# A decoder layer on one core: first values for all columns at once, the order of the last loads of v, and a last norm shared with TensorE

## The chip, the cores and the metric

The kernel runs on one core of one Trainium2 chip. The metric is the device time of one execution in microseconds (us); of several runs the median is given.

## The reference

One decoder layer on 256 tokens of width 2048, in float32. The weights are large, the tokens few.

```python
dq, dk, dv, sq, sk, sv = split(x @ w_in)              # 2048 x 6144
merged = concat(diff_attention(dq, dk, dv),           # 8 heads, rotary, two softmaxes
                stick_breaking_attention(sq, sk, sv)) # 8 heads
x = layer_norm(alpha * x + merged @ w_out)
x = layer_norm(alpha * x + peer_ffn(x))               # 16384 experts: gelu(x . u[e]), times v[e]
x = layer_norm(alpha * x + sigmoid(x @ w_gate) * (p @ w_proj))
```

`layer_norm` is `(x - mean) * rsqrt(var + eps) * g + b` over the 2048 columns.

## The kernel before, in words

**Layout.** P is 128 partitions, T 256 tokens, NT = 2 token tiles t, ND = 16 tiles k of the model's width d. `X` holds x transposed, tile by tile, as a high part and a low part (float32r each, side by side), so that a product in float32 precision is three fast products: `mm3` (L218) does hi x wh (L221), hi x wl (L222), lo x wh (L223), each 128x512.

**Weights.** Class `Stage` loads a weight tile `wf` with a DMA on SP's queue (`load`, L101), and splits it (`split`, L108): ACT casts the high part `wh` (L114), DVE subtracts to get the low part `wl` (L115). Buffers go round: 4 of `wf` and 4 pairs of `wh`, `wl` in the attention stage, each 1024 columns wide; a load waits until the buffer's last reader is done.

**First values.** The kernel begins with the values of the stick-breaking heads, `values(2, before=load_x)` (L370, L315): 1024 columns, c = 0 and then c = 1, 512 columns each. For each c, `gemm_N` (L225) goes over 8 pairs of d tiles; a load of 128x1024 holds both tiles of a pair for these 512 columns, and a pair gives 12 products. Two PSUM banks hold c's sums for the two token tiles, and ACT copies them out at the end of each c (L324). While c = 0 runs, x is loaded too: `load_x0` (L255) for tiles 0 and 1, one at a time, `load_x` (L261) for the later pairs; ACT makes the high part (L258, L264) and DVE the low one (L259, L265). The first pair of weights comes in two halves (`halves`, L118). All these DMAs stand in SP's queue: x tile 0, half of w, x tile 1, half of w, then x and w by pairs. `load_constants` follows c = 0.

**The middle.** Query and key projections (`proj`, `gemm_T`, L202 and L204) with attention in between, the output projection, the first norm, the expert queries (L214), then 128 blocks of u (`u_block`, L973) and twice 128 blocks of v (`v_block`, L1054), each block a 128x1024 or 128x2048 tile of weights. Beside them 200 gathers of expert rows run on POOL's DMA queue, and `gate_work` (L908) makes one-hot matrices: DVE compares, ACT scales (L929, L930), PE multiplies (L937, L938), DVE applies. The framework's scheduler places these pieces between the blocks; only what is passed to `keep` stays in program order.

**The end of v.** The last STAG = 6 blocks of v (three loads of 1 MB) are held and used j by j (L1150 to L1182), so that sums, transposes and statistics of the second norm fit in between. The loop at L1150 issues the held loads of v (`v_load`) and two loads of the gate's weights, the first after v's block 123, the second after 127. All share five buffers of 1 MB in the pool `sup`. `parts0` splits the gate's first weights (L1154). Then come the second norm (`ln_stats`, L477; POOL takes the reciprocal root, L482) and the gate's 4 column chunks. `gate_out` (L1256) loads the embedding through POOL's queue (L1260), applies the sigmoid (L1264), the product (L1265), the sum (L1266) and the statistics (L1269).

**The last norm.** `finish_stats` (L1272) combines the statistics; POOL takes the reciprocal root `rstd` (L1277). `pass1` (L1283) computes (x - mean) * g and `pass2` (L1288) x * rstd + b, both on DVE over column cuts, and after each piece of `pass2` SP issues the output's DMA (L1292). For token tile 1 this comes behind PE's last product, with cuts of 640, 640, 512 and 256 columns.

Of the kernel before, what the change touches and what calls it, by code (L numbers as in the profile page):

```python
# [9 lines left out]
F32 = mybir.dt.float32  # L10
# [9 lines left out]
P = 128  # L20
T = 256
NT = T // P
D = 2048
# [37 lines left out]
OHB = 5  # L61
STAG = 6
WF = 5

# [23 lines left out]
class Stage:  # L88
# [19 lines left out]
    def split(self, wf, c0, n=None):  # L108
# [7 lines left out]
        return wh, wl  # L116

    def halves(self, src, before):  # L118

        wf = self.wf_pool.tile([P, 1024], F32, name="wf", tag="wf", bufs=self.wf_bufs)  # L120
        for j in range(2):
            c = slice(j * 512, j * 512 + 512)
            before(j)
            self.nc.sync.dma_start(wf[:, c], src[:, c])
            yield self.split(wf, j * 512, 512)

# [36 lines left out]
def build(tc, a, out):  # L163
# [60 lines left out]

    def gemm_N(st, src, xt, pairs, pss, first=True, last=True, before=None):  # L225

        pairs = list(pairs)
        for i in pairs:
            if before and i:
                before(i)  # L230
            k = 2 * i
            parts = st.parts(src(i)) if i or not before else st.halves(src(i), load_x0)
            for wh, wl in parts:
# [21 lines left out]
    def load_x0(k):  # L255
        xf = sap.tile([P, T], F32, name="xf0", tag="xf0", bufs=2)
        nc.sync.dma_start(xf, a["xT"][:, k, :])
        nc.scalar.copy(X[:, k, :T], xf)  # L258
        nc.vector.tensor_tensor(X[:, k, T:], xf, Xf[:, k, :T], op=ALU.subtract)  # L259
# [54 lines left out]

    def values(base, before=None):  # L315
        v = cap.tile([P, NT, HEADS * HD], F32, name="v", tag="v", bufs=2)
        for c in range(2):
            pss = [pbank(pp, "ps_v") for _ in range(NT)]
            gemm_N(sa, lambda i: a["w_v"][base + c, i], X, range(ND // 2), pss,
                   before=before if c == 0 else None)  # L320
            if before and c == 0:
                load_constants()
            for t in range(NT):
                nc.scalar.copy(v[:, t, c * 512:(c + 1) * 512], pss[t])  # L324
        return v
# [43 lines left out]

    vs_ = values(2, before=load_x)  # L370
    for h in range(HEADS):
# [78 lines left out]

    vd_ = values(0)
    x1 = [x1p.tile([P, D], F32, name=f"x1_{t}") for t in range(NT)]
# [686 lines left out]
    for ia in range(SEG1, NIA - STAG):  # L1139
# [139 lines left out]

    def cuts(cut):  # L1280
        return [slice(*p_) for p_ in zip([0] + cut, cut + [D])]

    def pass1(t, cut, mv, rstd):  # L1283
        for s in cuts(cut):
            keep(nc.vector.scalar_tensor_tensor(x2[t][:, s], x2[t][:, s], mv[:, 0:1], gr3[:, s],
                                                op0=ALU.subtract, op1=ALU.mult))

    def pass2(t, cut, mv, rstd):  # L1288
        for s in cuts(cut):
            keep(nc.vector.scalar_tensor_tensor(x2[t][:, s], x2[t][:, s], rstd, br3[:, s],  # L1290
                                                op0=ALU.mult, op1=ALU.add))
            nc.sync.dma_start(out[t * P:(t + 1) * P, s], x2[t][:, s])  # L1292
# [83 lines left out]
    for c in range(NCH):  # L1376
        if c == NCH - 1:
            pass2(0, [512, 1024, 1536], *mr)
            gate_out(c, 1, ps_half, 256, 256)
            break  # L1380
# [19 lines left out]
        mr = finish_stats(0)  # L1400
        pass1(0, [512, 1024, 1536], *mr)
# [52 lines left out]
def _layout(inp):  # L1454
# [6 lines left out]
    def pairs(q, k):  # L1461
# [49 lines left out]
```

## Time and profile before

| | us |
|---|---|
| median of three runs (1776.26 to 1778.22) | 1777.45 |
| the profiled execution | 1776.11 |
| its span, first to last instruction | 1774.2 |
| PE busy | 1752.7 |
| first product on PE | 4.57 |
| first product of the query and key projections | 53.25 |
| last product of the gate ends | 1762.9 |

How to read it: times in the trace count from the span's start. PE is TensorE's products, PEld its weight loads, DVE VectorE, ACT ScalarE, POOL GpSimd; SPq, ACTq and POOLq are instructions that issue DMAs. A line of the timeline has the start, the duration, engine, source line, operation, output<-input, shapes, count, and in brackets the idle time before it and what ended it. A line of the chain has start, duration and what. In the list of waits stand the total, the number and the longest.

### The profile page before, as it was taken

How to read it: one execution, taken by the hardware profiler on the slowest of the kernel's cores; microseconds unless marked ns; L12 is line 12 of the kernel's file. 1: busy time of each engine (PE TensorE's matmuls, PEld its weight loads, DVE VectorE, ACT ScalarE, POOL GpSimd, SP SyncE). 2: the span in 40 equal slices, each digit the busy share in tenths (PEclk: the TensorE clock that was granted, in tenths of full speed). 3: DMA queues.
4: the chain of work that ended last, by engine and by line, in shares of the span. 5: the costliest groups of instructions: out<-in, count | busy, mean ns of one | idle time of the engine just before them, and what ended most of it. 6: DMA issues, size and time to landing. Idle time of an engine off the chain costs nothing.

```text
span 1774.2 us, 30337 instructions
## 1 busy us (share of the span) xinstructions
PE 1752.7 (99%) x12074; PEld 1647.6 (93%) x12074; DVE 1058.7 (60%) x1699; ACT 540.3 (30%) x1347; POOL 516.4 (29%) x554
## 2 busy tenths in 40 slices
PE   8999999999999999999999999999999999999997
PEld 6888888888889999999999999999999999999786
DVE  5565588664699877345655644876343433344686
ACT  5677468742110100104333313651000000000452
POOL 0143033105346227323333333333223232321000
PEclk9999999999999999999999999999999999999998
DMA  7544644576998999999999999999999999999671
GB/s 284 193 158 163 232 159 145 178 270 219 381 419 309 421 416 417 421 421 420 420 421 413 419 419 418 405 420 397 421 421 420 421 421 420 420 420 405 216 267 59
DMA packets 99822, 606.22 MB, mean 342 GB/s; under 512 B 12824, under 2 KB 14544, under 8 KB 35776
## 3 DMA queue, kind: packets, MB, share of 16 engines
q1 hardware_dynamic: 68368, 388.82, 55.4%
q0 software_dynamic: 30160, 213.10, 29.3%
q8 instruction: 95, 1.56, 0.4%
q10 hardware_dynamic: 1152, 2.36, 0.4%
q14 instruction: 47, 0.39, 0.1%
HBM read 598.36 MB, written 6.03 MB: 341 GB/s over the span
## 4 chain that ended last, share of the span: by engine, by line
PE 93%; DMA 4%; DVE 1%; ACT 0%; issue 0%; SPq 0%; POOL 0%; DVEq 0%; ACTq 0%
PE ps_v L1043 30%; PE ps_u L214 29%; PE ps_qk L202 7%; PE ps_q L214 6%; PE ps_qk L204 4%; DMA wf<-peer_u 2%; PE ps_v L222 2%; PE ps_v L223 2%; PE ps_gate L221 2%; PE ps_gate L223 2%; PE ps_gate L222 2%; PE ps_v L221 2%; DMA wf<-peer_v 1%; PE ps_mix L222 1%; PE ps_mix L223 1%; PE ps_mix L221 1%
## 5 line engine op out<-in xcount | busy, mean ns | idle before, releaser
L1043 PE MATMUL ps_v<-A,wf 128*128 128x156 f32 x4096 | 553.0, 297 | 1.2 <-DMA wf<-peer_v 1.1
L1043 PEld LDWEIGHTS ps_v<-A,wf 128*128 128x128 f32 x4096 | 545.0, 190 | 2.7 <-DMA wf<-peer_v 1.9
L214 PE MATMUL ps_u<-XF,wf 128*128 128x156 f32 x3904 | 528.2, 297 | 1.8 <-DMA wf<-peer_u 1.3
L214 PEld LDWEIGHTS ps_u<-XF,wf 128*128 128x128 f32 x3904 | 519.2, 190 | 3.1 <-ACT A L976 2.0
L841 DVE SCALAR_TENSOR_TENSOR y<-gb,ew,y 128x2048 f32<-128x2048 f32 x94 | 220.9, 2350 | 220.9 <-DMA gb<-v_rows,eig 220.7
L831 DVE SCALAR_TENSOR_TENSOR gb<-gb,xq 128x2048 f32<-128x2048 f32 x100 | 231.7, 2321 | 147.2 <-DMA gb<-u_rows,eig 147.1
L115 DVE TENSOR_TENSOR wl<-wf,wh 128x1024 fp32r<-128x1024 f32 (+1 forms) x199 | 212.7, 1090 | 110.5 <-ACT wh L114 98.9
L862 POOL COPY pace<-mark 1x1 f32<-1x1 f32 x200 | 108.2, 541 | 514.6 <-DMA mark<-c_iota 514.2
L114 ACT CAST wh<-wf 128x1024 fp32r<-128x1024 f32 (+1 forms) x199 | 172.1, 892 | 142.2 <-PE ps_yn L887 30.3
L202 PE MATMUL ps_qk<-X,wh 128*128 128x512 f32 x512 | 185.2, 401 | 0.0
L976 ACT ACTIVATE A<-ps_u 128x156 f32<-128x156 f32 x128 | 38.4, 300 | 433.6 <-PE ps_u L214 361.9
L864 POOL DMA_INDIRECT gb<-v_rows,eig x100 | 137.2, 1372 | 90.1 <-DVE y L841 54.7
L864 POOL DMA_INDIRECT gb<-u_rows,eig x100 | 122.1, 1221 | 126.3 <-DVE gb L831 67.2
L204 PE MATMUL ps_qk<-X,wl 128*128 128x256 f32 x512 | 145.7, 285 | 0.0
L929 ACT ACTIVATE hi<-eq,ghf 128x64 f16<-128x64 f16 x312 | 104.8, 336 | 45.1 <-DVE eq L923 42.2
L202 PEld LDWEIGHTS ps_qk<-X,wh 128*128 128x128 f32 x512 | 96.4, 188 | 21.9 <-issue 1.0
L214 PE MATMUL ps_q<-XF,wf 128*128 128x256 f32 x512 | 113.6, 379 | 0.6 <-DVE XF L509 0.6
L1104 ACT COPY x<-ps_y 128x256 f32<-128x256 f32 (+3 forms) x12 | 5.2, 439 | 346.3 <-DVE st L1103 346.1
L214 PEld LDWEIGHTS ps_q<-XF,wf 128*128 128x128 f32 x512 | 95.9, 190 | 13.1 <-DVE XF L509 0.8
L930 ACT ACTIVATE lo<-eq,glf 128x64 f16<-128x64 f16 x312 | 104.4, 335 | 0.0
L204 PEld LDWEIGHTS ps_qk<-X,wl 128*128 128x128 f32 x512 | 96.3, 188 | 2.5 <-issue 1.3
L947 DVE SCALAR_TENSOR_TENSOR A<-ps_G,A 128x30 f32<-128x30 f32 (+2 forms) x96 | 32.5, 368 | 45.0 <-PE ps_G L938 39.5
(261 smaller groups left out, 1801.0 us busy)
## 6 DMA issues: line engine op xcount, KB each, us to landing
wf<-peer_v SPq DMA_DIRECT2D x128, 1024.0 KB
wf<-peer_u SPq DMA_DIRECT2D x122, 1024.0 KB
wf<-w_qk SPq DMA_DIRECT2D x64, 512.0 KB
wf<-w_out SPq DMA_DIRECT2D x32, 512.0 KB
wf<-peer_wq SPq DMA_DIRECT2D x16, 1024.0 KB
wf<-ple_gate SPq DMA_DIRECT2D x16, 1024.0 KB
wf<-w_v SPq DMA_DIRECT2D x31, 512.0 KB
early<-peer_u SPq DMA_DIRECT2D x6, 1024.0 KB
```

The lines of the kernel that those rows point to most:

```text
L114: self.order(nc.scalar.copy(wh, src))
L115: self.order(nc.vector.tensor_tensor(wl, src, wh.bitcast(F32), op=ALU.subtract))
L202: nc.tensor.matmul(ps, wh[:, j * P:(j + 1) * P], xt[:, dt, :], start=dt == 0, stop=False)
L204: nc.tensor.matmul(ps[:, :T], wl[:, j * P:(j + 1) * P], xt[:, dt, :T], start=False, stop=dt == ND - 1)
L214: nc.tensor.matmul(ps[:, :T - t0], wf[:, dt * P:(dt + 1) * P], xt[:, dt, t0:], start=dt == 0, stop=dt == ND - 1)
L831: keep(nc.vector.scalar_tensor_tensor(g, g, 1.0, xq[i], op0=ALU.mult, op1=ALU.mult, accum_out=eact[i][:, j:j + 1]))
L841: keep(nc.vector.scalar_tensor_tensor(ys[i], g, ew[i][:, j:j + 1], ys[i], op0=ALU.mult, op1=ALU.add))
L862: keep(nc.gpsimd.tensor_copy(pace, mark))
L864: keep(nc.gpsimd.indirect_dma_start(out=g, out_offset=None, in_=a[kind], in_offset=bass.IndirectOffsetOnAxis(ap=eig[i][:, 0, j:j + 1], axi ...
L929: nc.scalar.mul(hi[:, j, :], eq[:, j, :], ghf[:, t])
L930: nc.scalar.mul(lo[:, j, :], eq[:, j, :], glf[:, t])
L1043: return nc.tensor.matmul(ps[:, (j % 2) * NDT:(j % 2 + 1) * NDT], vf[:, j * P:(j + 1) * P], W_of(ia), start=False, stop=ia == NIA - 1 and ...
```

## The change

Three places change.

1. `first_values` takes the place of `values(2, ...)`. It goes over the 16 d tiles once; for each it loads 128x1024 weights, all columns of that tile, from a new layout `w_sv`, and does the 12 products of both c into four PSUM banks (two of `pp`, two of `pt_`). x's tiles 0 and 1 are loaded through ACT's DMA queue, the weights and later pairs of x through SP's. Ahead of it, NZERO = 3 products of a zeroed part of M into a bank of its own go to PE. The constants follow tile 8, and the four copies of the sums stand at the end.
2. The gate's first two loads come after all held loads of v.
3. In the last norm of token tile 1, `pass1` goes over quarters, the last two first. For these two, PE computes `first_row.T @ b` (a row of b on all partitions; the same product is issued twice, and the second one starts the sum anew) and adds `diag(rstd) @ x`; ACT builds the diagonal, copies the sum out of PSUM and issues the output's DMA. `pass2` on DVE keeps the first two quarters. Token tile 0 keeps its four quarters.

In PE's order the four products with `first_row` stand behind the gate's last product; in POOL's order three loads of `gate_out` stand ahead of the second norm's reciprocal roots.

```diff
     def load_x0(k):
         xf = sap.tile([P, T], F32, name="xf0", tag="xf0", bufs=2)
-        nc.sync.dma_start(xf, a["xT"][:, k, :])
+        nc.scalar.dma_start(xf, a["xT"][:, k, :])
+        yield
         nc.scalar.copy(X[:, k, :T], xf)
         nc.vector.tensor_tensor(X[:, k, T:], xf, Xf[:, k, :T], op=ALU.subtract)
...
+    def first_values():
+        v = cap.tile([P, NT, HEADS * HD], F32, name="v", tag="v", bufs=2)
+        x0 = [load_x0(k) for k in range(2)]
+        for x in x0:
+            next(x)
+        nc.vector.memset(Mf[:, 0, :T], 0.0)
+        ps = pbank(pt_, "ps_zero", "o", 1)
+        for _ in range(NZERO):
+            nc.tensor.matmul(ps[:, :T], Mf[:, 0, :P], Mf[:, 0, :T], start=True, stop=True)
+        pss = [[pbank(pp, "ps_v") for _ in range(NT)],
+               [pbank(pt_, "ps_v", "s", 2) for _ in range(NT)]]
+        for k in range(ND):
+            if k == 0:
+                wf = sap.tile([P, 1024], F32, name="wf", tag="wf", bufs=4)
+                for c in range(2):
+                    nc.sync.dma_start(wf[:, c * 512:(c + 1) * 512],
+                                      a["w_sv"][0][:, c * 512:(c + 1) * 512])
+                next(x0[0], None)
+                parts = [sa.split(wf, c * 512, 512) for c in range(2)]
+            else:
+                if k > 1 and k % 2 == 0:
+                    load_x(k // 2)
+                wf = sa.load(a["w_sv"][k])
+                if k == 1:
+                    next(x0[1], None)
+                wh, wl = sa.split(wf, 0)
+                parts = [(wh[:, c:c + 512], wl[:, c:c + 512]) for c in (0, 512)]
+            for c in range(2):
+                for t in range(NT):
+                    mm3(pss[c][t], X, k, t, *parts[c], k == 0, k == ND - 1)
+            if k == ND // 2:
+                load_constants()
+        for c in range(2):
+            for t in range(NT):
+                nc.scalar.copy(v[:, t, c * 512:(c + 1) * 512], pss[c][t])
+        return v
...
-    vs_ = values(2, before=load_x)
+    vs_ = first_values()
...
-    held, gw = [], []
+    held = []
     for ia in range(NIA - STAG, NIA):
         held.append(v_load(1, ia))
-        if ia in (NIA - STAG + 1, NIA - 1):
-            gw.append(sg2.load(a["ple_gate"][0, len(gw)]))
+    gw = [sg2.load(a["ple_gate"][0, i]) for i in range(2)]
     parts0 = [sg2.split(gw[0], c * 512) for c in range(4)]
...
+    first_row = l2.tile([P, P], F32, name="first_row")
+    nc.gpsimd.memset(first_row, 0.0)
+    nc.gpsimd.memset(first_row[:1], 1.0)
...
-    mr = finish_stats(1)
-    pass1(1, [640, 1280, 1792], *mr)
-    pass2(1, [640, 1280, 1792], *mr)
+    psf = [pbank(pp, "ps_fin") for _ in range(2)]
+    for again in range(2):
+        for ps, s in zip(psf, quarters[2:]):
+            keep(nc.tensor.matmul(ps, first_row, br3[:, s], start=True, stop=not again))
+    mv, rstd = finish_stats(1)
+    diag = l3.tile([P, P], F32, name="diag")
+    keep(nc.scalar.mul(diag, ident, rstd))
+    pass1(1, quarters[2:] + quarters[:2], mv, rstd)
+    for ps, s in zip(psf, quarters[2:]):
+        keep(nc.tensor.matmul(ps, diag, x2[1][:, s], start=False, stop=True))
+        keep(nc.scalar.copy(x2[1][:, s], ps))
+        nc.scalar.dma_start(out[P:, s], x2[1][:, s])
+    pass2(1, quarters[:2], mv, rstd)
...
-        "w_v": _row_chunks(np.concatenate([dv, sv], axis=1)),
+        "w_v": _row_chunks(dv),
+        "w_sv": sv.reshape(ND, P, HEADS * HD),
```

More of the change, by code (lines that the diff above doesn't have):

```diff
@@ L62 @@
 STAG = 6
+NZERO = 3
 WF = 5
@@ L116, in split @@
         return wh, wl
[L118 to L125, printed above, removed]
     def parts(self, src):
@@ L223, in mm3, with gemm_N @@
         order(nc.tensor.matmul(ps, lo, wh, start=False, stop=stop))
-    def gemm_N(st, src, xt, pairs, pss, first=True, last=True, before=None):
+    def gemm_N(st, src, xt, pairs, pss, first=True, last=True):
         pairs = list(pairs)
         for i in pairs:
-            if before and i:
-                before(i)
             k = 2 * i
-            parts = st.parts(src(i)) if i or not before else st.halves(src(i), load_x0)
-            for wh, wl in parts:
+            for wh, wl in st.parts(src(i)):
                 for j in range(wh.shape[-1] // 512):
@@ L312, in load_constants2, with values @@
         nc.vector.tensor_scalar_mul(subg, subg, 1.0 - LAMBDA_INIT)
-    def values(base, before=None):
+    def first_values():
[34 more added lines that the diff above has]
+        return v
+    def values():
         v = cap.tile([P, NT, HEADS * HD], F32, name="v", tag="v", bufs=2)
@@ L318, in values @@
             pss = [pbank(pp, "ps_v") for _ in range(NT)]
[L319 to L322, printed above, removed]
+            gemm_N(sa, lambda i: a["w_v"][c, i], X, range(ND // 2), pss)
             for t in range(NT):
@@ L449, in diff_attention @@
         split_into(M, h, od, 0, T)
-    vd_ = values(0)
+    vd_ = values()
     x1 = [x1p.tile([P, D], F32, name=f"x1_{t}") for t in range(NT)]
@@ L1278, in finish_stats @@
         return mv, rstd
-    def cuts(cut):
-        return [slice(*p_) for p_ in zip([0] + cut, cut + [D])]
+    quarters = [slice(c * 512, (c + 1) * 512) for c in range(NCH)]
     def pass1(t, cut, mv, rstd):
-        for s in cuts(cut):
+        for s in cut:
             keep(nc.vector.scalar_tensor_tensor(x2[t][:, s], x2[t][:, s], mv[:, 0:1], gr3[:, s],
@@ L1288, in pass2 @@
     def pass2(t, cut, mv, rstd):
-        for s in cuts(cut):
+        for s in cut:
             keep(nc.vector.scalar_tensor_tensor(x2[t][:, s], x2[t][:, s], rstd, br3[:, s],
@@ L1377, in build @@
         if c == NCH - 1:
-            pass2(0, [512, 1024, 1536], *mr)
+            pass2(0, quarters, *mr)
             gate_out(c, 1, ps_half, 256, 256)
```

2 lines of the change are left out of this document (1 added, 1 removed).

## The prediction

> **What bounds the kernel now.** I read the page first: the busy shares and the chain of work that ended last.
>
> ```profile
> span 1774.2 us, 30337 instructions
> PE 1752.7 (99%) x12074; PEld 1647.6 (93%) x12074; DVE 1058.7 (60%) x1699; ACT 540.3 (30%) x1347; POOL 516.4 (29%) x554
> PE 93%; DMA 4%; DVE 1%; ACT 0%; issue 0%; SPq 0%; POOL 0%; DVEq 0%; ACTq 0%
> ```
>
> PE works for 1752.7 of 1774.2 us, and 93% of the chain is PE. So only two things can be gained: the 21.5 us in which PE is idle, and work that PE does too slowly. The second view is PE's list of waits, which says where that idle time is.
>
> ```profile
> PE ps_v L221 <- ACT wh L114: 4.9, 2, 4.6
> PE ps_u L214 <- DMA wf<-peer_u: 1.3, 3, 0.5
> PE ps_v L1043 <- DMA wf<-peer_v: 1.1, 1, 1.1
> PE ps_u L214 <- ACT A L976: 0.4, 1, 0.4
> ```
>
> The reader is to see how short it is: 4.9 us at the start, 1.1 us on one load of v, little else. The rest lies behind PE's last product, in the last norm. The change works at exactly these three places, so I take them one by one in the timeline and hold the other 1700 us to be unchanged.
>
> **Part 1, the first values.** The timeline and the chain of the first 12 us, then the first product of the next stage:
>
> ```profile
> 2.95 0.40 ACT L258 CAST X<-xf 128x256 fp32r<-128x256 f32 x1 [0.94 <-DMA xf<-xT]
> 1.18 0.42 SPq L124 DMA_DIRECT2D wf<-w_v  x1
> 3.90 0.62 ACT L114 CAST wh<-wf 128x512 fp32r<-128x512 f32 x1 [0.55 <-DMA wf<-w_v]
> 4.57 1.22 PE L221 MATMUL ps_v<-wh,X 128*128 128x512 f32 x2 [4.57 <-ACT wh L114]
> 6.18 0.62 ACT L114 CAST wh<-wf 128x512 fp32r<-128x512 f32 x1 [1.36 <-DMA wf<-w_v]
> 9.01 0.63 PE L222 MATMUL ps_v<-wl,X 128*128 128x512 f32 x1
> 9.44 0.63 PE L223 MATMUL ps_v<-wh,X 128*128 128x512 f32 x1
> 3.06 6.17 DMA wf<-w_v
> 9.26 1.04 ACT L114 CAST wh<-wf 128x1024 fp32r<-128x1024 f32 x1 [0.73 <-DMA wf<-w_v]
> 10.34 1.22 DVE L115 TENSOR_TENSOR wl<-wf,wh 128x1024 fp32r<-128x1024 f32 x1 [1.08 <-ACT wh L114]
> 11.62 0.51 PE L222 MATMUL ps_v<-wl,X 128*128 128x512 f32 x1 [0.33 <-DVE wl L115]
> 12.12 0.23 PE ps_v L223
> 53.25 0.39 PE L202 MATMUL ps_qk<-X,wh 128*128 128x512 f32 x1
> ```
>
> The phase has 192 products. The first twelve start 0.43 us apart (9.01 to 9.44), the later ones 0.23: PE begins at half rate and is at full rate when it comes back after 10.4. At 11.62 fourteen are issued; the other 178 take 53.25 - 11.62 = 41.63 us, 0.234 each. What decides is therefore when the third step can run: the second pair of d tiles is loaded in 6.17 us (issued 3.06, landed 9.23), cast in 1.04, its low part made in 1.22, and only then PE runs without a gap.
>
> How many bytes had to move for that comes from windows that begin at zero (the last two columns are the busy share of the DMA engines and GB/s):
>
> ```profile
> 0.00:6.15 6.15, 1.58 (x4) 1.25 (x5) 1.45 (x3) 2.61 (x4) 0.32 (x6) 1.00 0.59 157
> 0.00:9.23 9.23, 4.66 (x11) 3.65 (x12) 2.81 (x5) 3.85 (x6) 0.32 (x6) 1.00 0.69 215
> 0.00:8.20 8.20, 3.63 (x9) 2.81 (x10) 2.15 (x4) 3.52 (x6) 0.32 (x6) 1.00 0.66 201
> ```
>
> Up to the load that decides, 1.54 MB stand in the queue (two 128 KB tiles of x, two 256 KB halves of w, 256 KB of x, 512 KB of w). By 9.23 us 215 x 9.23 = 1.98 MB had moved: 0.45 MB of later loads ran beside it. In the new order twelve products need one d tile of all 1024 columns: 0.77 MB before the first tile is complete (two x, two halves of w), and 1.28 MB until the second tile's weights are there, since its x came with the first. With the same 0.45 MB beside it that is 1.73 MB; 201 x 8.20 = 1.65 MB had moved by 8.20, so it lands at about 8.4 (w's first issue also moves up from 1.18 to x's old place, which I count for nothing beyond that).
>
> From there: cast to 9.45, low part to 10.7, then the tile's last eight products, 8 x 0.234, to 12.6, and fourteen more tiles of twelve: 12.6 + 168 x 0.234 = 51.9. The two tiles behind it need 0.77 and 0.51 MB more at some 400 GB/s, less time than PE's 2.8 us for each, so they are not late. **The term is 53.25 - 51.9 = 1.35 us.** PE's first real product doesn't move: ACT now casts the weights first and x second, and w lands half a microsecond sooner, about 3.4 + 0.62 + 0.40 = 4.4 against 4.57.
>
> Ends for the unknown: if the load lands when it did (9.23), the sum is 0.5; if it lands when the queue has moved 1.28 MB and nothing beside it (7 us), PE is held by its own twelve products and the gain is 2.6.
>
> The **zero products** are three of 128x256 in fp32. The nearest row is the queries':
>
> ```profile
> L214 PE MATMUL ps_q<-XF,wf 128*128 128x256 f32 x512 | 113.6, 379 | 0.6 <-DVE XF L509 0.6
> ```
>
> 512 records are 256 products, so one is two records of 0.222 us at full rate, and at half rate, by the ratio 0.43 to 0.234, 0.82 us. Three take 2.5 us, from about 1.1 (after the memset) to 3.6: inside PE's idle 4.57 us, free. If they started over 0.9 us later they would push the first real one. What they can give is an earlier full rate. In my sum that matters little, since the load at 8.4 holds PE: at full rate from some 7 us on, PE has done its first tile by about 8.8 and waits.
>
> [...]
>
> Four copies of v instead of two now stand at the end of the phase on ACT, four times 0.59 by this row:
>
> ```profile
> L324 ACT COPY v<-ps_v 128x512 f32<-128x512 f32 x3 | 1.8, 588 | 2.2 <-PE ps_v L223 2.1
> ```
>
> In ACT's new order three casts of the next weights come ahead of them, each worth about 2.8 us of PE's work, so 2.4 us of copies are covered threefold; without that cover they would cost at most 2.4.
>
> **Part 2, v's last loads.** SP's timeline, the chain, and PE, ACT and POOL behind them:
>
> ```profile
> 1629.10 0.33 SPq L104 DMA_DIRECT2D wf<-ple_gate  x1
> 1633.34 4.57 SPq L104 DMA_DIRECT2D wf<-peer_v  x2
> 1637.58 6.36 DMA wf<-peer_v
> 1643.98 0.80 PE L1043 MATMUL ps_v<-A,wf 128*128 128x156 f32 x4 [1.13 <-DMA wf<-peer_v]
> 1645.05 2.18 ACT L114 CAST wh<-wf 128x512 fp32r<-128x512 f32 x4 [30.31 <-PE ps_yn L887]
> 1663.37 1.76 PE L1043 MATMUL ps_v<-A,wf 128*128 128x156 f32 x12
> 1668.04 1.11 POOL L482 TENSOR_TENSOR ln_rstd<-ln_rstd,half_neg 128x1 f32<-128x1 f32 x2 [45.96 <-DVE ln_neg L486]
> 1669.10 1.75 POOL L1260 DMA_DIRECT2D em<-s_emb  x3
> ```
>
> A load of the gate's weights is issued at 1629.10 between v's; v's last is issued at 1637.58, lands at 1643.94, and PE stands 1.13 us. In the new order v's last two take the places of 1629.10 and 1633.34. The load issued at 1633.34 was there when PE needed it (before 1642.85, since PE did not stop earlier), so the stop goes whole: **1.1 us**. What is late next? The gate's load now holds the place of 1637.58 and lands near 1643.94, just when ACT, 1.1 us earlier, wants to cast it; its products come 26 us later, so even some microseconds of delay stay covered. Bounds: 1.13 and, if that cast and DVE's subtractions behind it hold up the residual's sums, 0.
>
> One thing is moved past POOL: three of `gate_out`'s loads now stand ahead of the two reciprocal roots of the second norm, on which PE waits. They wait for v's last products, which end at 1665.1, and take 1.75 us: 1666.9 against 1668.04. Both move up together; there is 1.1 us of room, so nothing.
>
> **Part 3, the last norm.** DVE, POOL and SP behind PE's last product, a product of that size, and two windows:
>
> ```profile
> 1765.19 2.73 DVE L1285 SCALAR_TENSOR_TENSOR x<-x,mv,g_row 128x640 f32<-128x640 f32 x4
> 1765.35 1.12 POOL L1277 TENSOR_TENSOR rstd<-rstd,half_neg 128x1 f32<-128x1 f32 x1 [9.35 <-DVE rstd L1276]
> 1768.74 2.29 SPq L1292 DMA_DIRECT2D out<-x  x4
> 1665.34 0.86 PE ps_emb L1122 x2
> 1766.00:1767.00 1.00, 0.00 (x0) 0.00 (x0) 1.00 (x3) 0.00 (x0) 0.47 (x1) 0.50 0.00 0
> 1770.00:1771.00 1.00, 0.00 (x0) 0.00 (x0) 0.57 (x2) 0.00 (x0) 0.00 (x0) 0.50 1.02 387
> ```
>
> Two of four quarters leave DVE's second pass (4 x 0.68 us) and go to PE. The root is ready at 1766.47; the diagonal takes ACT about 0.4, a product 0.86, the copy 0.59: the first such quarter is out at 1768.5, the second at 1769.5 behind an issue of 0.33. DVE's two are out at 1768.6 and 1769.3. So the last issue falls from 1770.6 (1768.74 + 2.29 less its own 0.4) to 1769.5. But 1 MB must still be written, and from 1770 the DMA engines are full (1.02 busy, 387 GB/s): 1.05 MB / 387 GB/s = 2.7 us after the first bytes. The first issue only moves from 1768.74 to about 1768.55. **The term is 0.2 us**; the ends are 1.1, the whole advance of the last issue, and a loss of 0.9, if PE's clock, 0.50 in the window at 1766, had fallen before the two diagonal products. The four products with `first_row` (4 x 0.86 us from 1762.9 to 1766.4) stand against that.
>
> **The sum.** 1.35 + 1.1 + 0.2 = 2.65 us off the profiled execution's 1776.11 (span 1774.2 and 1.9 around it): 1773.5. That execution lies 1.3 below the median of the runs shown, 1777.45; against the median I predict **1774.8**.
>
> **Rivals.** (a) The first loads hide it: the order of the queue changes, but the slow first 8 us of DMA (157 GB/s up to 6.15) belong to the start, not to the bytes, and the second tile lands at 9.2. Part 1 gives 0.5: 1775.6. For it: that rate is at a busy share of only 0.59. Against: by 9.23 the queue was ahead by 0.45 MB. (b) The gain is larger: the load lands at 7, and the tail follows the last issue: 2.6 + 1.1 + 1.1 = 4.8: 1772.7. (c) The zero products don't bring the full rate forward: it comes at 10.4 as before. The first tile's twelve then last from 4.5 to 9.7, 9.9 with the wait for w's second half; one more product runs at 0.43 and the next at 0.234, and the second tile ends at 13.0 instead of 12.6. 0.95 + 1.1 + 0.2: 1775.2. For it: PE is idle again from 3.6 to 4.5. Against: PE's work begins 3.5 us sooner than before. [...] (d) Slower: the changed start lets the scheduler place the one-hot products of the gates elsewhere between the blocks of u and v. In PE's new order many stand one or two blocks away from where they stood. One that comes before its scalings holds PE, and with it all that follows, for a group of ten scalings of 0.336 us:
>
> ```profile
> L929 ACT ACTIVATE hi<-eq,ghf 128x64 f16<-128x64 f16 x312 | 104.8, 336 | 45.1 <-DVE eq L923 42.2
> ```
>
> That is 3.4 us each; one eats the whole gain, two make it slower, 1777.45 + 2 x 3.4 - 2.65 = 1781.6. Against it: the list of waits has 0.4 us on ACT in that stage, and the new order keeps nearly the same distance between scalings and products.
>
> **Chances.** Forecast 0.45, (a) 0.15, (b) 0.20, (c) 0.13, (d) 0.07. A measurement of this kernel can tell about 0.2%, 3.6 us, from no change. Below 1773.9 lie (b) and a good quarter of the forecast's own spread: faster 0.32. Above 1781 lies (d): slower 0.07. The rest, 0.61, is within. The range takes in the bounds of parts 1 and 3 and 1 us of the runs' own spread: 1771.8 to 1777.8.
>
> **What would show it.** In the changed profile: the first product of q and k near 51.9; PE's wait on peer_v gone and the gate's first cast near 1642.6, 2.45 us earlier; full-rate products before 9 us; the last SP and ACT issues near 1767 with DMA full for 2.7 us behind the first. I am wrong if PE's waits in the blocks of u and v grow by more than 1 us, or if the first stage ends later than 53.

## The result, and the profile after

| us | before | after |
|---|---|---|
| median of the runs beside each other | 1777.11 | 1773.07 |
| the profiled execution | 1776.11 | 1771.9 |
| its span | 1774.2 | 1770.1 |

The ratio is 0.9978, with an interval of 0.9972 to 0.9985: 4.0 us faster in the medians, 2.7 to 5.0 by the interval. The forecast was 2.65, which is where the interval begins, so the measured gain is the larger one. The median, 1773.07, lies within the stated range (1771.8 to 1777.8), but below 1773.9, under which the prediction saw a gain clear of noise, with a chance of 0.32 against 0.61 for less. The profiled executions differ by 4.0 us in span (1774.16 and 1770.13 to a hundredth). Cut at the three places of the change, that difference is: 2.03 up to the first product of the query and key projections (53.25 to 51.22), 1.69 from there to the first product `ps_yn` behind v's last loads (1591.26 to 1589.57 us long), 0.07 up to the gate's last sigmoid, and 0.24 from there to the end (11.25 to 11.01).

The page of after, first: span, busy times and the chain.

```profile
span 1770.1 us, 30377 instructions
PE 1758.6 (99%) x12092; PEld 1650.8 (93%) x12092; DVE 1058.2 (60%) x1698; ACT 541.7 (31%) x1350; POOL 527.4 (30%) x556
PE 95%; DMA 3%; DVE 1%; issue 1%; ACT 0%; POOL 0%; POOLq 0%; ACTq 0%; SPq 0%; DVEq 0%
```

PE's busy time rises by 5.9 us while the span falls by 4.0. That is no contradiction: the zero, first-row and diagonal products (2.92, 3.60 and 1.98 us in PE's timeline) stand where PE was idle before. A busy sum can't be read as progress here. PE's waits:

```profile
PE ps_zero L315 <- DVE M L312: 1.2, 1, 1.2
PE ps_u L206 <- DMA wf<-peer_u: 1.2, 3, 0.5
PE ps_v L213 <- ACT X L248: 1.2, 1, 1.2
...
PE ps_fin L1443 <- ACT diag L1440: 0.5, 1, 0.5
```

The wait on peer_v is gone, those in the blocks of u have not grown. At the start 1.2 + 1.2 us stand in place of 4.9. Lines of the start from the timelines of PE, ACT and SP:

```profile
0.73 0.90 ACTq L246 DMA_DIRECT2D xf<-xT  x2
0.74 0.87 SPq L322 DMA_DIRECT2D wf<-w_sv  x2
1.19 2.92 PE L315 MATMUL ps_zero<-M 128*128 128x256 f32 x6 [1.19 <-DVE M L312]
4.30 0.62 ACT L115 CAST wh<-wf 128x512 fp32r<-128x512 f32 x1 [1.35 <-DMA wf<-w_sv]
4.82 0.40 ACT L248 CAST X<-xf 128x256 fp32r<-128x256 f32 x1
5.27 1.22 PE L213 MATMUL ps_v<-wh,X 128*128 128x512 f32 x2 [1.16 <-ACT X L248]
6.89 1.04 ACT L115 CAST wh<-wf 128x1024 fp32r<-128x1024 f32 x1 [0.57 <-DMA wf<-w_sv]
8.86 0.63 PE L214 MATMUL ps_v<-wl,X 128*128 128x512 f32 x1
9.28 0.44 PE L215 MATMUL ps_v<-wh,X 128*128 128x512 f32 x1
9.56 0.39 PE L214 MATMUL ps_v<-wl,X 128*128 128x512 f32 x1
10.02 1.08 PE L213 MATMUL ps_v<-wh,X 128*128 128x512 f32 x4
```

Three things are to be seen. The zero products end at 4.1, and 1.2 us of idle time follow. The first real product comes at 5.27, later than before (4.57) and than forecast (4.4). And the products start 0.42 us apart until 9.28, 0.23 from 9.56 on, with no gap between them: after 5.27 PE waits for no load; its own half rate is the limit. The second d tile's weights were there in time, cast at 6.89 and needed at 10.02.

### The profile page after: what moved, and what is told of

It is laid out like the page before. It is cut to its first block, busy times and chain, and to the rows that moved or that the text cites. A ratio compares the mean times of both kernels' runs of the same rounds, so it can differ in the third digit from the quotient of the medians.

```text
span 1770.1 us, 30377 instructions
## 1 busy us (share of the span) xinstructions
PE 1758.6 (99%) x12092; PEld 1650.8 (93%) x12092; DVE 1058.2 (60%) x1698; ACT 541.7 (31%) x1350; POOL 527.4 (30%) x556
## 4 chain that ended last, share of the span: by engine, by line
PE 95%; DMA 3%; DVE 1%; issue 1%; ACT 0%; POOL 0%; POOLq 0%; ACTq 0%; SPq 0%; DVEq 0%
PE ps_v L1069 31%; PE ps_u L206 29%; PE ps_qk L194 7%; PE ps_q L206 6%; PE ps_qk L196 4%; DMA wf<-peer_u 2%; PE ps_v L213 2%; PE ps_v L215 2%; PE ps_v L214 2%; PE ps_gate L213 1%; PE ps_gate L215 1%; PE ps_gate L214 1%; PE ps_mix L214 1%; PE ps_mix L215 1%; PE ps_mix L213 1%
## 5 line engine op out<-in xcount | busy, mean ns | idle before, releaser
L888 POOL COPY pace<-mark 1x1 f32<-1x1 f32 x200 | 122.3, 612 | 528.6 <-DMA mark<-c_iota 527.4
L890 POOL DMA_INDIRECT gb<-u_rows,eig x100 | 126.6, 1266 | 125.6 <-DVE gb L857 67.6
L890 POOL DMA_INDIRECT gb<-v_rows,eig x100 | 130.0, 1300 | 65.7 <-DVE y L867 28.8
```

Of the source, the lines that this page charges most:

```text
L888: keep(nc.gpsimd.tensor_copy(pace, mark))
L890: keep(nc.gpsimd.indirect_dma_start(out=g, out_offset=None, in_=a[kind], in_offset=bass.IndirectOffsetOnAxis(ap=eig[i][:, 0, j:j + 1], axi ...
```

## The experiments

Each run's ratio is to runs of the kernel before on the same chip. Since the effects are about 1 us and the medians of one kernel differ by as much, I read the times together with four moments of each profiled execution: the first product of q and k (start), the stretch to the first `ps_yn` (middle), and the stretch from the gate's last sigmoid to the end (tail). Full rate is where products (or records of the zero products) begin to start some 0.23 us apart instead of 0.42. In every trace the record of the granted TensorE clock begins at this moment, and the column gives that beginning. Start, middle and tail are differences of times in the trace; the tail takes the span to a hundredth, where the recorded expectations took it to a tenth (10.98 there is 11.01 here).

| kernel | ratio, interval | full rate at | start | middle | tail |
|---|---|---|---|---|---|
| before | 1 | 10.8 | 53.25 | 1591.26 | 11.25 |
| after | 0.9978, 0.9972 to 0.9985 | 9.4 | 51.22 | 1589.57 | 11.01 |
| e1_values | 0.9983, 0.9974 to 0.9992 | 10.6 | 51.79 | 1591.20 | 11.26 |
| e2_vorder | 0.9992, 0.9983 to 1.0001 | 9.4 | 52.30 | 1591.32 | 11.24 |
| e3_norm | 0.9998, 0.9989 to 1.0007 | 10.7 | 52.15 | 1591.92 | 10.86 |
| e4_zero0 | 0.9985, 0.9976 to 0.9994 | 9.1 | 51.35 | 1590.11 | 11.02 |
| e5_zero5 | 0.9970, 0.9958 to 0.9982 | 6.5 | 50.06 | 1590.75 | 11.05 |
| e5_zero8 | 0.9977, 0.9966 to 0.9987 | 4.4 | 50.28 | 1589.71 | 11.01 |
| e6_xsp | 0.9980, 0.9971 to 0.9990 | 10.7 | 52.08 | 1588.45 | 10.77 |
| e7_row1 | 0.9974, 0.9964 to 0.9984 | 9.9 | 51.43 | 1589.69 | 11.03 |
| e8_order4 | 0.9979, 0.9970 to 0.9988 | 5.6 | 51.77 | 1589.49 | 10.86 |
| e8_order5 | 0.9982, 0.9973 to 0.9991 | 7.1 | 51.48 | 1590.45 | 10.86 |
| e9_old5 | 0.9987, 0.9978 to 0.9996 | 4.2 | 52.65 | 1591.01 | 10.86 |
| e10_tail | 0.9970, 0.9959 to 0.9981 | 4.4 | 49.70 | 1588.79 | 10.63 |

### Each part alone, and no zero products

My theory was that of the prediction: three terms that add, the start's from the order of the loads. Against it stood that the moment of full rate decides the start, whatever the loads do, and that the last issue sets the end.

e1_values has the new `first_values` alone:

```diff
-    gw = [sg2.load(a["ple_gate"][0, i]) for i in range(2)]
+        if ia in (NIA - STAG + 1, NIA - 1):
+            gw.append(sg2.load(a["ple_gate"][0, len(gw)]))
...
-    pass1(1, quarters[2:] + quarters[:2], mv, rstd)
...
+    pass1(1, cuts, *mr)
+    pass2(1, cuts, *mr)
```

> Part 1 alone (first values by d tile with the zero products; the loads of v and the last norm as before). Theory A (the three gains are separate and add up): the first product of q and k comes near 51.2 instead of 53.25, and the whole execution is 2.0 us shorter than before, +-0.8. Rival B (the blocks of u and v, where the DMA engines are full, give it back): the first stage still ends near 51.2, but the execution is less than 1 us shorter. The wait on v's last load stays at about 1.1 us by both.

e2_vorder has the new order of v's loads alone:

```diff
-    vs_ = first_values()
+    vs_ = values(2, before=load_x)
...
-    pass1(1, quarters[2:] + quarters[:2], mv, rstd)
...
+    pass1(1, cuts, *mr)
+    pass2(1, cuts, *mr)
```

> Part 2 alone (v's last loads ahead of the gate's). Theory A: PE's wait on peer_v (1.13 us) is gone, nothing else waits, 1.1 to 1.4 us shorter than before. Rival B: the gate's first load, now the later one, holds ACT's first cast of the gate's weights and the time behind it; the wait moves there and the execution is within 0.4 us of before.

e3_norm has the new last norm alone:

```diff
-    vs_ = first_values()
+    vs_ = values(2, before=load_x)
...
-    gw = [sg2.load(a["ple_gate"][0, i]) for i in range(2)]
+        if ia in (NIA - STAG + 1, NIA - 1):
+            gw.append(sg2.load(a["ple_gate"][0, len(gw)]))
```

> Part 3 alone (half of the last second pass on TensorE). Theory A (the last megabyte is written at the rate of the DMA engines, so an earlier last issue gives little): from PE's last gate product to the span's end 0.2 to 0.4 us less than before's 11.3. Rival B (the last issue decides): 1.0 us less, since the last issue comes a microsecond earlier.

e4_zero0 has all three, without the zero products:

```diff
-NZERO = 3
+NZERO = 0
```

> All three parts, but no zero products (0 instead of 3; they compute nothing that the output needs). Theory A (PE's early work brings its full rate forward): full rate comes at 10.4 or later instead of 9.3, and the first product of q and k comes at 51.7 to 52.5 instead of 51.2. Rival B (the change of rate depends on where it falls after the first real product, or on chance): full rate near 9.3 and the first stage ends within 0.2 us of 51.2.

Medians, against 1777.19 of before beside them: 1774.42 (e1), 1775.27 (e2), 1777.21 (e3), 1774.29 (e4). Part 1 alone is faster beyond its interval; for parts 2 and 3 alone the interval takes in no change. In the traces each part moves its own column. Start: 53.25, 52.30 and 52.15 with the old order (mean 52.57), 51.79, 51.22 and 51.35 with the new one, so some 1.1 us, and 2.03 in the first pair of traces was partly the scatter of the start itself (e1 missed the 51.2 that was expected, with its full rate at 10.6). Tail: 11.25, 11.26 and 11.24 with the old norm, 11.01, 10.86 and 11.02 with the new one: 0.3. Part 2 by the wait that it takes away, from the lists of waits of e1, e3 and e2:

```profile
PE ps_v L1069 <- DMA wf<-peer_v: 1.6, 1, 1.6
```

```profile
PE ps_v L1044 <- DMA wf<-peer_v: 1.4, 1, 1.4
```

```profile
PE ps_v L1044 <- DMA wf<-peer_v: 0.3, 1, 0.3
```

With the old order the wait is 1.1 to 1.6 us, with the new one 0 (after) to 0.6 (e5_zero5): about 1.1. The column "middle" shows no more than that it agrees: with the new order it lies between 1588.45 and 1591.32, a scatter of 2.9 us in which 1.1 us alone would not be seen.

e4 is the surprise. Without any zero product the full rate came at 9.1 us, no later than with three. PE's timeline of e4:

```profile
5.72 1.22 PE L213 MATMUL ps_v<-wh,X 128*128 128x512 f32 x2 [5.72 <-ACT X L248]
...
8.44 0.94 PE L215 MATMUL ps_v<-wh,X 128*128 128x512 f32 x2
9.22 0.39 PE L214 MATMUL ps_v<-wl,X 128*128 128x512 f32 x1
```

So the three zero products do nothing that these runs can tell, while the half rate is what bounds the start. Either zero products can't bring it forward, or three are too few since PE stands idle behind them.

### Five and eight zero products

e5_zero5 as below, e5_zero8 with 8.

```diff
-NZERO = 3
+NZERO = 5
```

> The changed kernel with five zero products instead of three. In the changed kernel three of them end near 4.1 us and the first real product starts at 5.27, all at half rate. Theory A (the rate rises only after an unbroken stretch of work; three are too few because 1.2 us of idle time follows them): five last to about 5.8 (1.19 + 5 x 0.9), so PE is busy from 1.2 on without a break, the 0.23 us pitch is there by some 6 to 8 us, and the first product of q and k starts at 50.4 to 50.8 instead of 51.2; time about 0.6 us under the changed kernel. [...]

> The changed kernel with eight zero products instead of three: at half rate they last to about 8.4 us, 3 us beyond the moment at which the first weights and x are there. Theory A (unbroken work brings the full rate): full rate by 5 to 7 us, the zero products end near 6.5 to 7.5, the first real product runs at 0.23 from its start, and the first product of q and k comes at 50.8 to 51.3. Rival B (the rate does not follow the zero products): real products start at about 8.4, still at half rate up to 9 to 10.6, and the first product of q and k comes at 52.5 to 53.5, so the time is 1.3 to 2.3 us above the changed kernel.

PE's timeline of e5_zero5, then of e5_zero8:

```profile
1.19 4.63 PE L315 MATMUL ps_zero<-M 128*128 128x256 f32 x10 [1.19 <-DVE M L312]
5.55 1.18 PE L213 MATMUL ps_v<-wh,X 128*128 128x512 f32 x2
6.56 0.63 PE L214 MATMUL ps_v<-wl,X 128*128 128x512 f32 x2
7.03 0.62 PE L213 MATMUL ps_v<-wh,X 128*128 128x512 f32 x2
```

```profile
1.18 5.31 PE L315 MATMUL ps_zero<-M 128*128 128x256 f32 x16 [1.18 <-DVE M L312]
6.14 0.81 PE L213 MATMUL ps_v<-wh,X 128*128 128x512 f32 x2
6.79 0.62 PE L214 MATMUL ps_v<-wl,X 128*128 128x512 f32 x2
```

No idle time stands in brackets at the first real product any more. In e5_zero5 pairs of products start 0.47 us apart from 6.56 on, so 0.23 each: full rate some 3 us earlier than in the changed kernel. In e5_zero8 sixteen records take 5.31 us, where ten took 4.63: the last ones ran at full rate already. The start ends at 50.06 and 50.28. Theory A holds in its direction: with work unbroken from 1.2 us on, the full rate came at 6.5 and 4.4 us. Both starts are earlier than the ranges that it had given (50.4 and 50.8 at the lower ends). Eight are too many: they still run when x and w are there, and the first real product starts at 6.14 instead of 5.55.

Why then, and not sooner or later? These runs don't settle it. Counted from the beginning of the last stretch of work (in before it has one pause of 0.3 us), the full rate came after 3.0 us (e9_old5, 1.19 to 4.23) to 6.2 us (before, 4.57 to 10.80). In the four traces with five zero products, all begun at 1.19 and with no pause before the change, it came at 4.2 (e9_old5), 4.4 (e10_tail), 6.5 (e5_zero5) and 7.1 us (e8_order5). Three zero products last 2.9 us (1.19 to 4.11), with 1.2 us of idle time behind them (1.6 in e6_xsp, below); in the four traces that have them (after, e1, e6, e7) the full rate came at 9.4 to 10.7 us, in e4 without any at 9.1.

### How the first loads are queued

Is the first real product, at 5.27 in spite of an early first issue, held by the two queues that load at once? e6_xsp puts x's first two tiles into SP's queue, ahead of the weights:

```diff
-        nc.scalar.dma_start(xf, a["xT"][:, k, :])
+        nc.sync.dma_start(xf, a["xT"][:, k, :])
```

> The changed kernel with the first two x tiles loaded through SP's queue, ahead of the weights, instead of through ACT's. In the changed kernel the first weights are cast at 4.30 although they were issued at 0.74, in the kernel before at 3.90 though issued at 1.18. Theory (loads of two queues share the DMA engines, so all of them land late together): in one queue x is there by about 3.2, the weights by 4.0 to 4.2, the first real product starts at 4.7 to 5.0 instead of 5.27, one product at half rate earlier, and the first product of q and k moves by 0 to 0.4 us, lost in the scatter of the full rate. Rival (the bytes ahead decide): the weights now stand behind 256 KB of x, are issued at about 1.5 and cast at 4.6 or later, the first real product at 5.4 or later, and the first product of q and k 0.2 to 0.5 us later.

The weights were cast at 4.99 and the first product came at 5.66: the rival's "5.4 or later". The start ended at 52.08, because here the full rate came only at 10.7: a start of the new order can be as late as the old one. (0.2 to 0.5 us later had been expected by the rival; it was 0.9, with the full rate's scatter in it.)

e8 takes the order of the kernel before (x tile 0, half of w, x tile 1, half of w, all on SP's queue) with four zero products (e8_order4, below) and five (e8_order5):

```diff
-NZERO = 3
+NZERO = 4
...
-        nc.scalar.dma_start(xf, a["xT"][:, k, :])
+        nc.sync.dma_start(xf, a["xT"][:, k, :])
...
-        for x in x0:
-            next(x)
+        next(x0[0])
...
                 for c in range(2):
+                    if c:
+                        next(x0[1])
```

> The changed kernel with four zero products, and its first loads in one queue in the order x tile 0, first half of w, x tile 1, second half of w (two queues, x on ACT's, before). Theory (with the full rate early, the start of the first real product decides, down to the limit that the second d tile's load sets): the first weights are cast at 3.9 to 4.3, the first real product starts at 4.7 to 5.1, the rate is full by 8 us at the latest, the second tile's low part is ready at about 9.3 and its last eight products end at 11.1, so the first product of q and k starts at 49.6 to 50.2 (five zero products gave 50.1 with the two queues); about 0.3 us under that kernel. Rival (the shared DMA engines make every first load as late as before, or four products leave a gap that restarts the slow stretch): first real product at 5.2 or later, or half rate to 9 us or beyond; first product of q and k at 50.5 to 51.5.

> The same order of the first loads with five zero products. Theory (an unbroken stretch of work from 1.2 us on brings the full rate by 4.6 to 8 us whatever the loads do): no idle time on PE after 1.2 us, first real product at 5.0 to 5.8 behind the zero products, first product of q and k at 49.7 to 50.2. Rival (the early full rate of the runs with five and eight zero products was the scatter that all starts show): half rate to 9 us or beyond, first product of q and k at 51 to 52.

The first half of the theory held, full rate at 5.6 and 7.1, and the first product at 4.97 and 5.26. Yet the start ended at 51.77 and 51.48, where 49.6 to 50.2 had been expected. ACT and PE of e8_order4 say why, and below them two windows of e8_order4, the same two of after, and those of e6_xsp with its cast of the second d tile (last columns of a window: granted clock, DMA share, GB/s):

```profile
6.94 0.62 ACT L115 CAST wh<-wf 128x512 fp32r<-128x512 f32 x1 [1.71 <-DMA wf<-w_sv]
7.61 0.73 PE L213 MATMUL ps_v<-wh,X 128*128 128x512 f32 x2 [0.69 <-ACT wh L115]
9.01 1.05 ACT L115 CAST wh<-wf 128x1024 fp32r<-128x1024 f32 x1 [1.45 <-DMA wf<-w_sv]
10.10 1.19 PE L213 MATMUL ps_v<-wh,X 128*128 128x512 f32 x4 [0.57 <-ACT wh L115]
```

```profile
5.00:6.00 1.00, 1.00 (x3) 0.77 (x4) 0.98 (x2) 0.22 (x1) 0.00 (x0) 1.00 0.73 236
6.00:7.00 1.00, 0.92 (x4) 0.39 (x3) 0.00 (x0) 0.06 (x1) 0.00 (x0) 1.00 0.78 262
```

```profile
5.00:6.00 1.00, 0.73 (x2) 0.63 (x3) 0.97 (x2) 0.82 (x3) 0.00 (x0) 1.00 0.93 372
6.00:7.00 1.00, 1.00 (x4) 0.81 (x3) 0.95 (x2) 0.43 (x3) 0.00 (x0) 1.00 1.03 391
```

```profile
5.00:6.00 1.00, 0.34 (x1) 0.34 (x2) 0.36 (x1) 0.73 (x2) 0.00 (x0) 1.00 1.01 363
6.00:7.00 1.00, 1.00 (x3) 0.61 (x3) 0.81 (x2) 0.49 (x1) 0.00 (x0) 1.00 0.99 350
7.41 1.04 ACT L115 CAST wh<-wf 128x1024 fp32r<-128x1024 f32 x1 [0.91 <-DMA wf<-w_sv]
```

With small and large loads in turn on one queue, w's second half is cast at 6.94 instead of 5.40 and the second d tile at 9.01 instead of 6.89, and now PE waits 0.69 and 0.57 us for them. In that stretch the engines moved 236 and 262 GB/s against 372 and 391 when ACT's queue carries x. Once the rate is full early, the loads are the limit again. Is it the second queue that the change gained? For the smaller part: e6_xsp has one queue too, but both tiles of x ahead of the weights, and it moved 363 and 350 GB/s and cast the second d tile at 7.41. So 1.6 us of the 2.1 between 9.01 and 6.89 go with loads of x and w in turn, and 0.5 with the single queue; each figure is from one pair of traces. The two traces of e8 and before have x and w in turn, and all stay below 265 GB/s in each microsecond from 4 to 7 us (189, 236 and 262 in e8_order4, 213, 213 and 236 in e8_order5, 150, 201 and 234 in before). Why the engines stand idle a quarter of the time there isn't settled by these runs.

### The old order with an early full rate

Would the zero products alone have done it? e9_old5 has the old first values, with five zero products, and the new parts 2 and 3:

```diff
-    vs_ = first_values()
+    vs_ = values(2, before=load_x)
...
+        if before:
+            nc.vector.memset(Mf[:, 0, :T], 0.0)
+            ps = pbank(pt_, "ps_zero", "o", 1)
+            for _ in range(NZERO):
+                nc.tensor.matmul(ps[:, :T], Mf[:, 0, :P], Mf[:, 0, :T], start=True, stop=True)
```

> The changed loads of v and the changed norm with the old order of the first values (the second step's two d tiles in one load, half of the columns first), and five zero products ahead of it. Theory (the order d tile by d tile is what lets the full rate count: in the old order the second step's load, landed at about 9.2, cast and subtracted by 11.5, holds PE whatever its rate): full rate by 8 us, but PE then waits 1 to 2 us for the second pair, and the first product of q and k stays at 52.1 to 53.2, as without zero products (52.15 to 53.25). Rival (only the rate counts, the order not): some ten products at 0.23 instead of 0.43 us, first product of q and k at 50.2 to 51.3, and the time as that of the changed kernel with five zero products.

Full rate at 4.2, and a start of 52.65, as late as without zero products. Its waits:

```profile
PE ps_v L222 <- ACT wh L115: 1.8, 2, 1.4
...
PE ps_v L223 <- DVE wl L116: 0.5, 1, 0.5
```

The second step's weights arrive, are cast at 9.44 and subtracted by 11.74, and PE, done early, waits 1.4 us for the cast and 0.5 for the low part; 0.4 us before that went to the first step's second half. The prediction's picture of the old start, "What decides is therefore when the third step can run", is shown right by this run. The parts of the new start need each other: the new loads without the early rate gained 1.1 us, the rate without the new loads nothing, both together 2.3 to 2.9 (from a mean of 52.57 to 50.28, 50.06 and 49.70). The order d tile by d tile alone isn't enough either: with the early rate, but x and w in turn on one queue, e8 gained 0.8 and 1.1.

### The last norm

e7_row1 runs the products with `first_row` once, so that PE pauses ahead of the diagonal products:

```diff
-    for again in range(2):
+    for again in range(1):
-            keep(nc.tensor.matmul(ps, first_row, br3[:, s], start=True, stop=not again))
+            keep(nc.tensor.matmul(ps, first_row, br3[:, s], start=True, stop=False))
```

> The changed kernel with the products of the first-row matrix run once instead of twice, so that PE stands still for about 2 us more ahead of the two diagonal products at the end. Theory (the repeat holds up the granted clock; the last megabyte's writing bounds the end anyway): the granted clock falls before the diagonal products and each takes up to twice its 0.99 us, the second quarter's copy ends up to 2 us later, but the first issues and the full DMA engines stay, so the stretch from the last gate's activation to the end grows from 10.98 us by 0.3 to 1.0 us. Rival (the clock does not fall that fast, or the copies have room): the stretch stays at 10.8 to 11.1 us. Time within 1 us of the changed kernel either way.

The timelines of PE, SP and ACT of after, then those of PE and ACT of e7_row1, and a window of e7_row1:

```profile
1763.03 1.98 PE L1443 MATMUL ps_fin<-x,diag 128*128 128x512 f32 x4 [0.51 <-ACT diag L1440]
1764.80 1.00 SPq L1320 DMA_DIRECT2D out<-x  x2
1765.83 0.35 ACTq L1445 DMA_DIRECT2D out<-x  x1
```

```profile
1763.37 2.88 PE L1443 MATMUL ps_fin<-x,diag 128*128 128x512 f32 x4 [2.24 <-ACT diag L1440]
1766.91 0.35 ACTq L1445 DMA_DIRECT2D out<-x  x1
```

```profile
1765.00:1766.00 1.00, 1.00 (x2) 0.00 (x0) 0.79 (x2) 0.17 (x1) 0.00 (x0) 0.50 0.03 12
```

The granted clock did fall (0.50; 1.00 in the same place of after), the four records took 2.88 us instead of 1.98, and the last issue came 0.74 us later behind the sigmoid (1766.91 - 1759.46 = 7.45 against 1765.83 - 1759.12 = 6.71). The end moved by 0.02 (11.03 against 11.01). So the last issue has 0.7 us of room and isn't what ends the kernel. The windows of after name what does:

```profile
1766.00:1767.00 1.00, 0.00 (x0) 0.00 (x0) 0.00 (x0) 0.00 (x0) 0.00 (x0) 1.00 1.01 375
1767.00:1768.00 1.00, 0.00 (x0) 0.00 (x0) 0.00 (x0) 0.00 (x0) 0.00 (x0) 0.61 1.04 379
```

The DMA engines are full. The packets say the same: in all fourteen traces the last output byte of token tile 1 lands 2.9 to 3.1 us after the first packet starts (2.99 in before, 3.00 in after), whether the last issue stands 7.7 us behind the sigmoid (before) or 6.7 (after). If so, only an earlier first issue helps. In e10_tail DVE finishes one quarter before it begins the next, with five zero products at the start:

```diff
-    pass1(1, quarters[2:] + quarters[:2], mv, rstd)
+    pass1(1, quarters[2:] + quarters[:1], mv, rstd)
+    pass2(1, quarters[:1], mv, rstd)
+    pass1(1, quarters[1:2], mv, rstd)
+    pass2(1, quarters[1:2], mv, rstd)
...
-    pass2(1, quarters[:2], mv, rstd)
```

> The changed kernel with five zero products, and at the end DVE writes its first quarter before it makes the second: first pass of quarters 3, 4, 1, second pass of 1, first pass of 2, second pass of 2, so that the first output is issued 0.68 us earlier, the last ones as before. Theory (the end is the moment of the first issue plus what the full DMA engines need for 1 MB, 2.7 us): the stretch from the last gate's activation to the end falls from 10.98 to 10.3 to 10.6 us. Rival (the last issue, ACT's of the second TensorE quarter, and its landing set the end): 10.9 to 11.05, unchanged. In time 0.3 to 0.7 us or nothing under five zero products alone.

SP's timeline of e10_tail, and its first window with output:

```profile
1762.18 1.78 SPq L1320 DMA_DIRECT2D out<-x  x2
```

```profile
1763.00:1764.00 1.00, 0.00 (x0) 0.00 (x0) 0.60 (x1) 0.58 (x1) 0.00 (x0) 1.00 1.01 373
```

The first issue stands 5.22 us behind the last sigmoid instead of 5.68, 0.46 earlier (DVE's instructions took 0.75 us each here, not 0.68 to 0.70), and the tail is 10.63 instead of 11.01, shorter than in the ten other traces of the new norm (10.77 to 11.05). That is 0.38 of the 0.46, just outside what the theory gave (10.3 to 10.6) and well off the rival. It is one trace beside a scatter of 0.3, but the packets bear it out: the last output byte lands 9.13 us behind the sigmoid, in those ten 9.42 to 9.54. This version has the lowest median, 1771.21 against 1777.31 of before. Its interval overlaps that of the changed kernel; that it is the better one is borne by its trace, a start of 49.70 and the shorter tail, not by the times.

## Why the prediction was right, and where not

**What bounds the kernel**: right. All that moved lies at the three places, apart from the scatter of the middle.

**Part 1, 1.35 us**: the size was close (1.1 over the starts, 2.03 in the first pair of traces), the reason was not. Three steps failed, and their errors cancel, so that the size came out close is luck.
- "lands at about 8.4": the second d tile's weights were cast at 6.89. The prediction kept the 0.45 MB that had run beside the old loads and the old queue's rate. e8_order4 shows that the old queue's order, x and w in turn, was itself slow (236 GB/s where x on ACT's queue gives 372). Taking x out of that sequence, for which the prediction had no term, was worth 2.1 us of landing time (6.89 against 9.01); e6_xsp has 1.6 of it with one queue.
- "about 3.4 + 0.62 + 0.40 = 4.4": the first real product came at 5.27. The weights' cast began at 4.30, after an earlier issue, and x's cast stood behind it until 5.22. 0.7 us were lost there against 4.57.
- "In my sum that matters little, since the load at 8.4 holds PE": the reverse. With the load early, PE's half rate up to 9.4 was the whole limit. The sign "full-rate products before 9 us" did not come. Rival (c), the zero products don't bring the full rate forward, was right, by e4 (9.1 us without any, 9.4 with three); e5_zero5 shows what two more of them bring: 51.22 to 50.06, 1.2 us. Its price, 0.95 us for part 1 instead of 1.35, was near the 1.1 measured. (The 10.4 us that the prediction read for the kernel before was the end of a wait; its full rate came at 10.8.)

**Rival (a)**, the slow first 8 us belong to the start and not to the bytes: refuted, by the windows of after at 372 GB/s from 5 us on. **Rival (b)**, a larger gain: its first condition came true, the load was there by 7 us, but its 2.6 us for part 1 were not reached, since the half rate held PE; the runs with an early full rate came to 2.3 to 2.9. Its second, that the tail follows the last issue, is refuted by e7. That its 1772.7 lies nearer to the measured 1773.07 than the forecast does is luck. **Rival (d)**, one-hot products misplaced: it did not happen, PE's waits in the blocks of u and v did not grow.

**Part 2, 1.1 us**: right. The wait is gone, the gate's first cast moved with it (1645.05 to 1641.33), and nothing was late next; in e2 and five other traces that cast did wait for the gate's load, and no wait of PE followed from it.

**Part 3, 0.2 us**: right, with 0.3 measured. The first issue moved by 0.15 behind the sigmoid (5.83 to 5.68), 0.19 had been forecast; the last one by 1.0, which gained nothing, as e7 shows. The end "a loss of 0.9" was not one: e7 lost the clock and lost 0.02.

**The sum**: 1.1 + 1.1 + 0.3 = 2.5 us by the mechanisms, 2.65 forecast, 2.7 to 5.0 measured. Of the 4.0 us between the first two traces, 0.9 is scatter of the start and 0.6 scatter of the middle. The medians are not one execution, and what lies above 2.5 in them no row explains: e1_values alone measured 1.4 to 4.6 us for a start that is 1.5 us earlier in its trace. The times are too wide to place the rest, and it stays open.

## What to carry to other kernels

At the start of this kernel two limits stood side by side, the loads (the second d tile cast at 6.89 us in after, 9.01 in e8_order4) and PE's half rate (products 0.42 us apart instead of 0.23, up to 9.4 us in after); moving one gained only up to the other (1.1 us for the loads, nothing for the rate, 2.3 to 2.9 for both), so experiments must move them one at a time and then together. Warm-up products brought the full rate forward here where four to eight of them, with or without the first real products, kept PE busy without a pause until then (4.2 to 7.1 us, in six traces); three of them and a pause of 1.2 us did nothing (9.4, against 9.1 with none). No run has more zero products with a pause behind them before the change, so a pause is not shown to be fatal by itself; in e9_old5 one of 1.4 us after the change left the rate full (products 0.23 us apart from 12.13 us on). At the end, ask which is full: where the last megabyte filled the DMA engines, as here (375 and 379 GB/s in after), the first issue counted (0.46 us earlier in e10_tail, and a tail shorter by 0.38), and faster last pieces bought nothing (the last issue 1.0 us earlier behind the sigmoid in after than in before, 0.74 later in e7 than in after with the end moved by 0.02).

## What the runs showed of the hardware

- With PE at work without a pause from 1.2 us on, the full rate came at 4.2, 4.4, 6.5 and 7.1 us in four traces with five zero products (e9_old5, e10_tail, e5_zero5, e8_order5), at 4.4 with eight (e5_zero8) and at 5.6 with four (e8_order4). In the eight traces with three or none, where the first real product starts at 4.57 to 5.72 us, it came at 9.1 to 10.8. What sets the moment within these ranges was not shown.
- The moment of full rate scatters from one execution to the next: 9.4, 9.9 and 10.6 us in three traces with the same start (after, e7, e1), whose query and key products begin at 51.22, 51.43 and 51.79. Each product at half rate took 0.2 us more (0.42 us between starts instead of 0.23).
- The granted clock reads 1.00 in the rows of the first 10 us, while products start 0.42 us apart instead of 0.23 (the window of after at 6.00 above). The column counts what is recorded as lost, and the record begins only with the full rate (at 9.35 in after). At this start the pitch of the products tells the rate, that column doesn't; at the end it did tell, 0.50 beside products that took longer (e7, four records in 2.88 us instead of 1.98).
- Between 5 and 7 us one queue with 128 KB and 256 KB loads in turn moved 236 and 262 GB/s (e8_order4), one queue with the 128 KB loads first 363 and 350 (e6_xsp), and two queues 372 and 391 (after).
